# Mixers' driver: a longer modelled wait ahead of each unit's second-chunk transposition

## The chip, the cores and the metric

One core of one Trainium2 chip runs the whole program. The metric is the device time of one execution in microseconds (us). The kernel before took 2300.38 us as the median of three runs (2298.58 to 2304.85).

## What is computed

Two transformer blocks on 256 tokens of width 2048, in float32. The first block begins with two mixers that share one input projection; their outputs are concatenated and projected. The mixers are where the change lies:

```python
xn = _rmsnorm(h, norm_mix[l])
y = xn @ w_in[l]
o_gdn = _gdn_group(y[..., :GDN_COLS], ...)      # gated delta rule, 8 heads of 128
o_rwkv = _rwkv_group(y[..., GDN_COLS:], ...)    # RWKV-7 scan, 16 heads of 64
h = h + jnp.concatenate([o_gdn, o_rwkv], axis=-1) @ w_out[l]
...
# _gdn_group, behind the recurrence: norm of each head, gain, gate
o = o * lax.rsqrt(jnp.mean(o * o, axis=-1, keepdims=True) + NORM_EPS)
o = o * norm_w.astype(jnp.float32) * jax.nn.silu(z)
# _rwkv_group, behind the recurrence: norm of each head, gain and bias, bonus, gate
o = ((o - mean) * lax.rsqrt(var + RWKV_GN_EPS)).reshape(B, T, W) * ln_w + ln_b
return (o + bonus.reshape(B, T, W)) * g
```

Cross attention, a squared-ReLU MLP and a second block with two kinds of attention follow; the change does not touch them.

## The kernel before, in words

**The two recurrences** are computed in chunks of 128 tokens (two chunks), each with a triangular inverse in place of the token loop. The work is cut into six units: four RWKV quarters of four heads (`rwkv_quarter`, here q0 to q3) and two GDN halves of four heads (`gdn_half`, here g0 and g1). They run in the order q0, q1, g0, q2, q3, g1. Every unit has three stages, divided by `yield None`:

- Stage 0 makes the decayed operands and the matrices to be inverted (`pn` in a quarter, `gram` in a half, both into `nt`).
- Stage 1 (`inverse_blocks`) inverts the 32x32 diagonal blocks on POOL: four DMAs to DRAM (`scr`), four back (`nb`), then 31 pairs of a product `Xt<-X,nb` and a sum `X<-X,Xt`.
- Stage 2 puts the inverse into place (`by_row`, `xd`; `inverse`, whose products are `py` and `pz`), and then does chunk 0 and chunk 1. In a quarter every head and chunk needs a product `lp`, whose copy is masked by two affine selects on POOL (tiles `p2a`, `p2b`, `p2c`, `og` for the four heads) before the product `rp` reads it. Then come `up` and `op`. The result of a chunk is normed: sums on DVE, the power -1/2 on POOL (`powc`, L182, tiles `var` in a quarter and `sso` in a half), and a product on DVE (`oc` in a quarter, `og` in a half). Last, `finish(c)` transposes the chunk on PE (`onp` in a quarter, `ot` in a half) into the tile `mix`.

**The order on PE** is written by the program itself (`manual_schedule`). A driver keeps a modelled clock `now`. Each unit is a generator; it issues some matmuls and yields two numbers, the PE time of what it issued and the wait until its next piece may be issued:

```python
now += r[0]
stage[q][1] = now + r[1]
```

While no unit's piece is due, the driver issues pieces of `main()`, the big projections, whose products are called `acc` here (a piece is six products of 128x256, or three of 128x512, and counts 0.66). At most two units may be ahead of the last stage, and a unit enters a stage when the one before it has left. `main()` also names what it needs: before the first column strip of the cross attention's key projection is copied out, it waits for `("end", "q3")`. Where nothing is due and `main()` may not go on, the driver only moves its clock on, and PE gets nothing between the two pieces.

**The order on the other engines** (DVE, ACT, POOL, SP) is made by a scheduler that estimates times and takes PE's order as given. Each of these engines executes its instructions in that fixed order: an instruction that is not ready holds back what stands behind it. Weights arrive in pieces through three buffers: a DMA to `raw` (L130), a copy `whi` on ACT (L99), a difference `wlo` on DVE (L135).

Of the kernel before, what the change touches and what calls it, by code (L numbers as in the profile page):

```python
# [63 lines left out]
def block_kernel(tc, a, out, dbg=None, stop=99):  # L64
# [30 lines left out]
    def mm(o, l, r, start=True, stop=True):  # L95
        nc.tensor.matmul(o, l, r, start=start, stop=stop)  # L96

    def act(o, i, f=AF.Copy, **kw):
        return nc.scalar.activation(o, i, f, **kw)  # L99

    def tt(o, x, y, op, eng=None):
        (eng or nc.vector).tensor_tensor(out=o, in0=x, in1=y, op=op)  # L102

    def ts(o, x, s1, op0, s2=None, op1=None, eng=None):
        if op1 is None:
            (eng or nc.vector).tensor_scalar(out=o, in0=x, scalar1=s1, scalar2=None, op0=op0)
        else:
            (eng or nc.vector).tensor_scalar(out=o, in0=x, scalar1=s1, scalar2=s2, op0=op0, op1=op1)
# [6 lines left out]
    def pst(shape, name):  # L115
        return PS["pool"].tile(shape, F32, name=name, tag="ps", bufs=8 - PS["mm"])
# [63 lines left out]
    def powc(o, i, e):  # L180

        nc.gpsimd.tensor_tensor(out=o, in0=i, in1=e, op=ALU.pow)  # L182
# [177 lines left out]
    def wk(shape, name, bufs=1, dt=F32):  # L360
        return work_p.tile(shape, dt, name=name, tag=name, bufs=bufs)
# [192 lines left out]
    def rwkv_quarter(qt):  # L554
# [107 lines left out]
        def lmat(c, h):  # L662

            i, e = h // 2, slice(64 * (h % 2), 64 * (h % 2) + 64)
            lp = pst([128, 3, 128], "lp")
            mm(lp[:, 0, :], BK[e, i, c, 0, :], AR[e, i, c, 1, :])
            mm(lp[:, 1:3, :], BK[e, i, c, 1, :], AR[e, i, c, :, :])
            l = wk([128, 3, 128], ("p2a", "p2b", "p2c", "og")[h])
            act(l[:, 0, :], lp[:, 0, :], scale=rn2[:, c, h:h + 1])
            act(l[:, 1:3, :], lp[:, 1:3, :])  # L670

            nc.gpsimd.affine_select(out=l[:, 1, :], in_=l[:, 1, :], pattern=[[1, 128]],
                                    compare_op=ALU.is_ge, fill=0.0, base=-1, channel_multiplier=-1)
            nc.gpsimd.affine_select(out=l[:, 0:3:2, :], in_=l[:, 0:3:2, :], pattern=[[0, 2], [1, 128]],
                                    compare_op=ALU.is_ge, fill=0.0, base=0, channel_multiplier=-1)
            L[h] = l
# [10 lines left out]
        def finish(c):  # L687
            onp = pst([128, 2, 128], "onp")
            for i in range(2):
                tr(onp[:, i, :], oc[c][:, 2 * i:2 * i + 2, :].rearrange("p h n -> p (h n)"))  # L690
            s = slice(c * 128, c * 128 + 128)
            for i, ct in enumerate(cts):
                act(m[:, i, s], onp[:, i, :], AF.Identity, scale=p_lw[:, ct:ct + 1], bias=p_lb[:, ct:ct + 1])
            tt(m[:, :, s], m[:, :, s], bon[:, :, s], ADD)
            tt(m[:, :, s], m[:, :, s], gT[:, :, s], MUL)

        for c in range(2):
            rp_ = pst([128, 4, 64], "rp_")
            for h in range(4):
                if c == 1 and h % 2 == 0:  # L700
                    mm(rp_[:, h:h + 2, :], AR[:, h // 2, 1, 0, :], zs[:, h // 2, :], stop=False)
                mm(rp_[:, h, :], L[h][:, 1, :], vtok[:, c, h, :], start=(c == 0), stop=(c == 0 or h % 2 == 1))
            rs = wk([128, 4, 64], "rs")
            act(rs, rp_)
            yield 0.45 + 0.4 * c, 1.3
            up = pst([128, 4, 64], "up")
            for h in range(4):
                mm(up[:, h, :], tinv[:, c * 4 + h, :], rs[:, h, :])
            us = wk([128, 4, 64], "us")
            nc.vector.tensor_copy(us, up)  # L710
            yield 0.45, 1.5
            op = pst([128, 4, 64], "op")
            for h in range(4):
                if c == 1 and h % 2 == 0:
                    mm(op[:, h:h + 2, :], AR[:, h // 2, 1, 1, :], zs[:, h // 2, :], stop=False)
                mm(op[:, h, :], L[h][:, 0, :], us[:, h, :], start=(c == 0), stop=False)
                mm(op[:, h, :], L[h][:, 2, :], vtok[:, c, h, :], start=False, stop=(c == 0 or h % 2 == 1))
            if c == 0:
                zp = pst([128, 2, 64], "zp")
                for h in range(4):  # L720
                    i, e = h // 2, slice(64 * (h % 2), 64 * (h % 2) + 64)
                    mm(zp[e, i, :], btok[:, h, :], us[:, h, :], stop=False)
                    mm(zp[e, i, :], ktok[:, h, :], vtok[:, 0, h, :], start=False)
                for h1 in range(2):
                    e = slice(64 * h1, 64 * h1 + 64)
                    tt(zs[e, :, e], zp[e], zsc[e].unsqueeze(2).to_broadcast([64, 2, 64]), MUL)

            mean = wk([128, 4], "mean", bufs=2)
            nc.vector.tensor_reduce(out=mean, in_=op, axis=AX.X, op=ADD)
            ts(mean, mean, 1.0 / 64, MUL)  # L730
            o_ = wk([128, 4, 64], "oc")
            oc.append(o_)
            tt(o_, op, mean.unsqueeze(2).to_broadcast([128, 4, 64]), SUB)
            osq = wk([128, 4, 64], "rs")
            act(osq, o_, AF.Square)
            var = wk([128, 4], "var", bufs=2)
            nc.vector.tensor_reduce(out=var, in_=osq, axis=AX.X, op=ADD)
            ts(var, var, 1.0 / 64, MUL, 64e-5, ADD)
            powc(var, var, mhalf[:, 0:4])
            tt(o_, o_, var.unsqueeze(2).to_broadcast([128, 4, 64]), MUL)  # L740
            if c == 0:
                yield 1.5, 0.5
                for h in range(4):
                    lmat(1, h)
                    yield 0.65, 0.4 if h < 3 else 2.5
                finish(0)
                yield 0.22, 0
            else:
                yield 0.9, 7.0
                finish(1)  # L750
                yield 0.22, 0
        done.add(("end", f"q{qt}"))
# [33 lines left out]
    def gdn_half(hf):  # L786
# [118 lines left out]
        def finish(c):  # L905
            p = pst([128, 4, 128], "ot")
            for i in range(4):
                tr(p[:, i, :], o_[c][:, i, :])
            act(mix[hf][:, :, c * 128:c * 128 + 128], p)
# [33 lines left out]
        tt(o_[1], p, o_[1], ADD)  # L943
        norm(1)
        done.add(("gq", hf))
        yield 2.2, 9.0
        finish(1)
        done.add(("gz", hf))
        yield 0.45, 0
# [3 lines left out]
    def main():  # L953
# [85 lines left out]
        for n in range(4):  # L1039
            def emit_v(t, p, n=n):  # L1040
# [6 lines left out]
    res = {}  # L1047

    queue = [(("r", 0), rwkv_quarter(0)), (("r", 0), rwkv_quarter(1)), (("q", 0, "in"), gdn_half(0)),
             (("r", 1), rwkv_quarter(2)), (("r", 1), rwkv_quarter(3)), (("q", 1, "in"), gdn_half(1))]  # L1050
    stage = [None, None, None]
    now, need, ms = 0.0, None, main()
# [439 lines left out]
```

## Time and profile before

| | |
|---|---|
| median of three runs | 2300.38 us |
| the profiled execution | 2295.65 us |
| its span in the trace | 2293.9 us |
| PE busy | 2234.1 us, 97% of the span |
| DVE, ACT, POOL busy | 1389.2, 1122.2, 264.1 us |
| mean granted TensorE clock | 0.989 |
| PE waiting before `onp` in all | 7.3 us, 3 times |
| PE waiting before `ot` in all | 3.7 us, 2 times |

PE is the engine that is nearly always at work, and the mixers' units lie between 100 and 625 us of the span. What counts there is each stretch in which PE stands still, and the clock that it is granted afterwards. A wait shown behind a row in square brackets is the time in which the engine sat idle before that row, with the instruction that ended it.

### The profile page before, as it was taken

What the parts mean: (1) busy time and instruction counts of PE and PEld (TensorE: products, weight loads), DVE (VectorE), ACT (ScalarE), POOL (GpSimd) and SP (SyncE); (2) the same over time, 40 slices, a digit from 0 to 9 for tenths busy, and PEclk for the clock granted to TensorE, in tenths of its full rate; (3) what the DMA queues carried; (4) which work ended last, traced back from release to release, by engine and by line L of the source; (5) the groups of instructions that cost most, each with busy time, mean ns of one, the idle gap of its engine ahead of it and who ended that gap; (6) DMA issues with size and microseconds to landing.
All of it is one profiled execution on the core that took longest, in us unless ns stands there. A gap on an engine that the chain in (4) does not pass through costs nothing.

```text
span 2293.9 us, 39047 instructions
## 1 busy us (share of the span) xinstructions
PE 2234.1 (97%) x15506; PEld 2024.6 (88%) x15506; DVE 1389.2 (61%) x2236; ACT 1122.2 (49%) x1802; POOL 264.1 (12%) x540
## 2 busy tenths in 40 slices
PE   8999999989999999999999999999999999999996
PEld 8998988878988899889998898899888999889975
DVE  6575676675654556555554455455456677778765
ACT  5454544554544445444454444344344565656542
POOL 0036164155100000000000000000000000011101
PEclk9999999999999999999999999999999999999998
DMA  6654344343466554466666666666656666665654
GB/s 208 184 160 122 93 132 137 105 147 104 141 213 207 182 180 148 142 188 184 185 186 188 188 188 188 186 190 185 187 185 201 201 189 185 182 180 168 180 181 133
DMA packets 229060, 391.77 MB, mean 171 GB/s; under 512 B 39886, under 2 KB 47820, under 8 KB 228493
## 3 DMA queue, kind: packets, MB, share of 16 engines
q1 hardware_dynamic: 227297, 385.63, 55.9%
q10 hardware_dynamic: 1036, 3.58, 0.4%
q8 instruction: 121, 1.98, 0.4%
q14 instruction: 62, 0.51, 0.1%
q0 software_dynamic: 544, 0.07, 0.0%
HBM read 386.25 MB, written 2.97 MB: 170 GB/s over the span
## 4 chain that ended last, share of the span: by engine, by line
PE 85%; POOL 6%; DVE 3%; DMA 2%; issue 2%; ACT 1%; SPq 0%; POOLq 0%; ACTq 0%; DVEq 0%
PE acc L96 77%; POOL Xt L102 3%; POOL X L102 2%; PE lp L96 1%; DVE wlo L135 1%; DMA nb<-scr 1%; PE s2p L96 1%; PE o2p L96 1%; PE tp L178 1%; PE t2p L178 1%; PE xo L96 0%; PE xs L96 0%; DVE h L111 0%; DVE xd L494 0%; PE op L96 0%
## 5 line engine op out<-in xcount | busy, mean ns | idle before, releaser
L135 DVE TENSOR_TENSOR wlo<-raw,whi 128x1024 fp32r<-128x1024 f32 (+1 forms) x696 | 853.7, 1228 | 717.2 <-ACT whi L99 714.0
L99 ACT ACTIVATE whi<-raw 128x1024 fp32r<-128x1024 f32 (+1 forms) x696 | 734.5, 1056 | 875.2 <-PE acc L96 759.5
L96 PE MATMUL acc<-ah,whi 128*128 128x256 f32 x3120 | 885.9, 284 | 2.2 <-DVE ey L102 2.0
L96 PE MATMUL acc<-al,whi 128*128 128x256 f32 x3120 | 875.3, 281 | 0.0
L96 PE MATMUL acc<-ah,wlo 128*128 128x256 f32 x3120 | 871.2, 280 | 1.1 <-DVE wlo L135 1.1
L96 PEld LDWEIGHTS acc<-ah,whi 128*128 128x128 f32 x3120 | 588.8, 189 | 10.9 <-issue 6.3
L96 PEld LDWEIGHTS acc<-al,whi 128*128 128x128 f32 x3120 | 588.2, 189 | 1.4 <-issue 0.9
L96 PEld LDWEIGHTS acc<-ah,wlo 128*128 128x128 f32 x3120 | 586.5, 188 | 2.0 <-DVE wlo L135 1.9
L96 PE MATMUL acc<-wlo,ah 128*128 128x512 f32 x704 | 278.9, 397 | 0.0
L96 PE MATMUL acc<-whi,al 128*128 128x512 f32 x704 | 278.7, 397 | 0.0
L96 PE MATMUL acc<-whi,ah 128*128 128x512 f32 x704 | 268.7, 402 | 4.0 <-DVE qky L102 2.6
L96 PE MATMUL acc<-wlo,uh 128*128 128x512 f32 x512 | 202.4, 395 | 0.0
L96 PE MATMUL acc<-whi,ul 128*128 128x512 f32 x512 | 202.3, 395 | 0.0
L96 PE MATMUL acc<-whi,uh 128*128 128x512 f32 x512 | 182.5, 395 | 0.0
L96 PEld LDWEIGHTS acc<-whi,ah 128*128 128x128 f32 x704 | 132.5, 189 | 34.6 <-DVE qky L102 2.8
L96 PEld LDWEIGHTS acc<-whi,al 128*128 128x128 f32 x704 | 132.7, 189 | 31.9
L96 PEld LDWEIGHTS acc<-wlo,ah 128*128 128x128 f32 x704 | 133.0, 189 | 30.1
L96 PEld LDWEIGHTS acc<-whi,ul 128*128 128x128 f32 x512 | 96.1, 188 | 23.3
L96 PEld LDWEIGHTS acc<-wlo,uh 128*128 128x128 f32 x512 | 96.0, 188 | 23.3
L96 PEld LDWEIGHTS acc<-whi,uh 128*128 128x128 f32 x512 | 95.9, 187 | 23.3
L102 POOL TENSOR_TENSOR Xt<-X,nb 128x60 f32<-128x60 f32 (+24 forms) x186 | 82.0, 441 | 181.6 <-DMA nb<-scr 160.9
L1335 POOL MEMSET klz<- 64x256 f32 x8 | 2.5, 307 | 714.9 <-DMA raw<-in_w_in_dram 714.6
(523 smaller groups left out, 1873.4 us busy)
## 6 DMA issues: line engine op xcount, KB each, us to landing
raw<-in_w_in_dram SPq DMA_DIRECT2D x240, 512.0 KB, 3.7
raw<-in_mlp_w_up_dram SPq DMA_DIRECT2D x128, 512.0 KB, 3.7
raw<-in_mlp_w_down_dram SPq DMA_DIRECT2D x128, 512.0 KB, 3.9
raw<-in_w_out_dram SPq DMA_DIRECT2D x64, 512.0 KB, 4.8
raw<-in_xattn_wk_dram SPq DMA_DIRECT2D x32, 512.0 KB, 4.2
raw<-in_xattn_wv_dram SPq DMA_DIRECT2D x32, 512.0 KB, 5.4
raw<-in_xattn_wq_dram SPq DMA_DIRECT2D x32, 512.0 KB, 4.0
raw<-in_xattn_wo_dram SPq DMA_DIRECT2D x32, 512.0 KB, 4.3
```

The lines of the kernel that those rows point to most:

```text
L96: nc.tensor.matmul(o, l, r, start=start, stop=stop)
L99: return nc.scalar.activation(o, i, f, **kw)
L102: (eng or nc.vector).tensor_tensor(out=o, in0=x, in1=y, op=op)
L135: last["dve"] = nc.vector.tensor_tensor(out=lo, in0=raw, in1=hi.bitcast(F32), op=SUB)
L178: nc.tensor.transpose(o, i, ident[0:n, 0:n])
L1335: nc.gpsimd.memset(kl[other, e, :].bitcast(F32), 0.0)
```

## The change

Two numbers of the driver's model: the wait between the last norm of a unit and the transposition of its second chunk goes from 7.0 to 10.0 in a quarter (L749) and from 9.0 to 13.0 in a half (L946).

```diff
@@ rwkv_quarter
             else:
-                yield 0.9, 7.0
+                yield 0.9, 10.0
                 finish(1)
                 yield 0.22, 0
@@ gdn_half
         done.add(("gq", hf))
-        yield 2.2, 9.0
+        yield 2.2, 13.0
         finish(1)
         done.add(("gz", hf))
```

No instruction is added or removed: what changes is the order. On PE the stretch of `acc` products between the last product of a unit's chunk 1 and its second transposition has these lengths (products before, now): q0 66, 96; q1 66, 96; g0 84, 120; q2 66, 96; q3 66, 42; g1 84, 120. At q3 it becomes shorter: `main()` comes to its need for q3's end, and the driver has nothing else to issue. Since a unit's end now comes later, the units behind it enter their stages later too, and the scheduler sorts the other engines anew. Two places follow on which the prediction rests.

POOL, from the second masked head of q3's chunk 0 on, before. `p2b`, `p2c` and `og` are the masked tiles of heads 1, 2 and 3; `wB` and `z` belong to g1, and `Xt<-X,nb` is the first step of g1's inversion.

```order
L672 AFFINE_SELECT p2b<-p2b 128x128
L674 AFFINE_SELECT p2b<-p2b 128x2x128
L102 TENSOR_TENSOR wB<-wB,cst 128x512
L672 AFFINE_SELECT p2c<-p2c 128x128
L674 AFFINE_SELECT p2c<-p2c 128x2x128
L672 AFFINE_SELECT og<-og 128x128
L674 AFFINE_SELECT og<-og 128x2x128
L102 TENSOR_TENSOR z<-z,normw 128x512
L102 TENSOR_TENSOR Xt<-X,nb 128x31
```

The same place now:

```order
L102 TENSOR_TENSOR wB<-wB,cst 128x512
L672 AFFINE_SELECT p2b<-p2b 128x128
L674 AFFINE_SELECT p2b<-p2b 128x2x128
L102 TENSOR_TENSOR Xt<-X,nb 128x31
L102 TENSOR_TENSOR X<-X,Xt 128x31
L102 TENSOR_TENSOR Xt<-X,nb 128x30
L102 TENSOR_TENSOR X<-X,Xt 128x30
L102 TENSOR_TENSOR Xt<-X,nb 128x29
L102 TENSOR_TENSOR X<-X,Xt 128x29
L672 AFFINE_SELECT p2c<-p2c 128x128
L674 AFFINE_SELECT p2c<-p2c 128x2x128
L102 TENSOR_TENSOR Xt<-X,nb 128x28
```

Before, all four heads were masked ahead of g1's inversion. Now six of its steps stand ahead of `p2c`, and twelve more ahead of `og`.

DVE, at the end of g0's chunk 1, before. The first row waits for the power of g0's norm on POOL; `og<-og,sso,z` are the four products that the transposition `ot` waits for; `xd` are copies of q2's inverse and `gv` belongs to a projection.

```order
L102 TENSOR_TENSOR sso<-sso,rqd 128x4
L494 COPY xd<-Xt 32x8x8 x6
L111 SCALAR_TENSOR_TENSOR gv<-ey,par_250,gv 128x254
L494 COPY xd<-Xt 32x8x8 x5
L111 SCALAR_TENSOR_TENSOR gv<-ey,par_250,gv 128x254
L111 SCALAR_TENSOR_TENSOR og<-og,sso,z 128x128 x2
L135 TENSOR_TENSOR wlo<-raw,whi 128x1024
L111 SCALAR_TENSOR_TENSOR og<-og,sso,z 128x128 x2
```

The same place now:

```order
L102 TENSOR_TENSOR sso<-sso,rqd 128x4
L135 TENSOR_TENSOR wlo<-raw,whi 128x1024
L111 SCALAR_TENSOR_TENSOR gv<-ey,par_250,gv 128x254
L111 SCALAR_TENSOR_TENSOR gv<-ey,par_250,gv 128x255
L111 SCALAR_TENSOR_TENSOR og<-og,sso,z 128x128 x4
L111 SCALAR_TENSOR_TENSOR gv<-ey,par_250,gv 128x253
```

The copies of q2's inverse now stand behind g0's four products instead of between them. In both orders the power of this norm stands on POOL behind all 62 steps of q2's inversion. The power of q2's own last norm stands behind 22 steps of q3's inversion (16 before), and that of q3's last norm behind all 62 steps of g1's, as before.

## Rows read from the trace of the kernel before

**Rows 1.** The page, busy time of each engine.

```profile
PE 2234.1 (97%) x15506; PEld 2024.6 (88%) x15506; DVE 1389.2 (61%) x2236; ACT 1122.2 (49%) x1802; POOL 264.1 (12%) x540
```

**Rows 2.** Waits of PE between 100 and 625 us: total, times, longest.

```profile
PE onp L178 <- DVE oc L102: 7.3, 3, 3.7
PE ot L178 <- DVE og L111: 3.7, 2, 2.6
PE rp__2783 L96 <- POOL og L672: 2.7, 1, 2.7
PE rp__2783 L96 <- POOL p2c L672: 2.2, 1, 2.2
```

**Rows 3.** Timeline of PE at the ends of q1, g0, q2, q3 (start, us).

```profile
308.64 0.44 PE L178 MATMUL onp<-cst,oc 128*128 128x128 f32 x2 [0.89 <-DVE oc L102]
...
396.69 0.59 PE L178 MATMUL ot<-cst,og 128*128 128x128 f32 x2 [2.63 <-DVE og L111]
398.36 0.74 PE L178 MATMUL ot<-cst,og 128*128 128x128 f32 x2 [1.07 <-DVE og L111]
...
463.99 0.69 PE L178 MATMUL onp<-cst,oc 128*128 128x128 f32 x2 [3.66 <-DVE oc L102]
...
552.01 0.39 PE L96 MATMUL op<-p2d,og 128*128 128x64 f32 x2
...
562.97 0.44 PE L178 MATMUL onp<-cst,oc 128*128 128x128 f32 x2 [2.75 <-DVE oc L102]
```

**Rows 4.** Timeline of POOL: steps of inversions (X, Xt) and powers (L182).

```profile
391.41 1.02 POOL L182 TENSOR_TENSOR sso<-sso,cst 128x4 f32<-128x4 f32 x1
...
455.34 0.24 POOL L102 TENSOR_TENSOR Xt<-X,nb 128x31 f32<-128x31 f32 x1 [13.37 <-DMA nb<-scr]
...
462.35 1.02 POOL L182 TENSOR_TENSOR var<-var,cst 128x4 f32<-128x4 f32 x1
...
530.27 0.24 POOL L102 TENSOR_TENSOR Xt<-X,nb 128x31 f32<-128x31 f32 x1 [2.81 <-DMA nb<-scr]
...
536.95 0.34 POOL L102 TENSOR_TENSOR X<-X,Xt 128x69 f32<-128x69 f32 x1
...
548.51 1.33 POOL L102 TENSOR_TENSOR X<-X,Xt 128x75 f32<-128x75 f32 x1
...
561.44 1.02 POOL L182 TENSOR_TENSOR var<-var,cst 128x4 f32<-128x4 f32 x1
```

**Rows 5.** Timeline of DVE at q3's chunk 1.

```profile
548.42 1.22 DVE L135 TENSOR_TENSOR wlo<-raw,whi 128x1024 fp32r<-128x1024 f32 x1
...
555.89 0.17 DVE L108 TENSOR_SCALAR var<-var 128x4 f32<-128x4 f32 x1
...
562.49 0.43 DVE L102 TENSOR_TENSOR oc<-oc,var 128x256 f32<-128x256 f32 x1 [4.27 <-POOL var L182]
```

**Rows 6.** Stretches: us, busy by engine, PEclk, DMA share, GB/s.

```profile
213.50:220.30 6.80, 5.25 (x24) 5.25 (x25) 0.26 (x1) 0.38 (x1) 5.33 (x21) 0.50 0.17 62
397.80:401.20 3.40, 2.84 (x13) 2.77 (x14) 3.34 (x9) 0.90 (x2) 0.00 (x0) 0.50 0.52 154
462.60:469.40 6.80, 5.41 (x26) 5.42 (x27) 2.60 (x4) 1.86 (x3) 5.86 (x14) 0.50 0.16 54
559.00:566.00 7.00, 4.25 (x37) 4.05 (x36) 3.51 (x9) 2.71 (x4) 2.83 (x10) 1.00 0.32 101
...
495.00:521.00 26.00, 23.28 (x222) 19.06 (x221) 22.39 (x66) 17.10 (x41) 9.39 (x10) 1.00 0.36 115
```

**Rows 7.** Timeline of PE at q3's chunk 0 and g1's last gram.

```profile
516.82 0.92 PE L96 MATMUL lp<-wA,wB 64*128 64x128 f32 x4
517.67 0.49 PE L96 MATMUL gram<-gk 128*128 128x128 f32 x2
...
525.87 0.33 PE L96 MATMUL rp__6514<-p2d,p2a 128*128 128x64 f32 x2
```

**Rows 8.** Waits of PE between 1750 and 2294 us: total, times, longest.

```profile
PE o2p L96 <- ACT ph L99: 2.6, 3, 1.1
```

## Prediction

> **What bounds the kernel now.** I read the page first: PE is busy for 97% of the span [rows 1], so time can be won almost only where PE stands still, or runs at the lower clock. The second view is the list of PE's waits in the mixers' stretch. The reader is to see there that the largest are exactly those that the change aims at: 7.3 us before `onp` and 3.7 us before `ot` [rows 2]. The next two belong to one place, the product `rp` of q0, which waited 2.2 and 2.7 us for masks on POOL. The third view is PE's timeline, which says where the 11 us lie: 0.89 us at the end of q1, 2.63 and 1.07 us at g0, 3.66 us at q2, 2.75 us at q3 [rows 3]. q0 and g1 have no wait there. The fourth is the timeline of POOL and DVE beside them. At q3 the sums of the norm are ready at 555.89 + 0.17 = 556.06 us [rows 5], but POOL raises them to their power only at 561.44 [rows 4], because the last steps of g1's inversion stand before it; DVE then lost 4.27 us on that power [rows 5]. At q2 the power stands behind 16 inversion steps, which begin when their DMA has landed at 455.34 and end at 462.35 [rows 4]. So what PE waits for is mostly POOL's queue. The last view is a table of stretches: after the waits at q0 (4.9 us), g0 (3.7) and q2 (3.66) the granted clock was 0.50, that is 1.2 GHz, for 6.8, 3.4 and 6.8 us, and after q3's 2.75 us it stayed at 1.00, 2.4 GHz [rows 6].
>
> **What the longer waits take away.** A product of 128x256 takes PE about 0.12 us here: from the last `op` pair at 552.01 to the point at which the wait before `onp` began, 562.97 - 2.75 = 560.22, PE did that pair and 66 of them in 8.21 us [rows 3]. 30 more are 3.6 us, 36 more are 4.4 us. This work stands in the order anyway; it is only drawn ahead, so it costs nothing by itself.
>
> - q0 and g1: no wait before, nothing won.
> - q1: 3.6 us against 0.89, -0.9.
> - g0: 4.4 us against 3.70, -3.7. Its power stands behind the whole of q2's inversion (sso at 391.41, [rows 4]), and q2 enters its stages later now. But on DVE the copies of q2's inverse have moved out of the way, which gives some of that back. Bounds: -3.7, or -1.5 if the power is 2 us later.
> - q2: 3.6 us against 3.66, and six of the products are twice as wide; -3.7. The six more steps before the power cost some 3 us of POOL (16 took 7.0 us), but the norm itself comes later on PE against q3's inversion. Bounds -3.7 and -1.
> - The stretches at the lower clock behind g0's and q2's waits go with them. PE was busy 2.84 and 5.41 us in them, and half of that is lost [rows 6]: -1.4 and -2.7.
>
> **q3, where the order does the opposite.** Here PE gets 42 products instead of 66, 2.9 us less. If nothing else moved, its wait would grow to 2.75 + 2.9 = 5.6 us. But something moves: g1's inversion now stands earlier against q3 on POOL. In the new order 18 of its 62 steps come before the last mask of chunk 0, and 12 are left behind the last mask of chunk 1, so I expect it to be over when q3's last norm comes. Then the sums at 556.06, a power of 1.02 us and a product of 0.43 us [rows 4, 5] give 557.5 on the scale of before, and PE arrives at 552.2 + 42 x 0.12 = 557.3. Left over 0.3 us: -2.5.
>
> **What comes in its place.** The masks of q3's heads 2 and 3 in chunk 0 now stand behind 6 and 18 steps of an inversion whose first step cannot begin before its DMA has landed. `rp` reads them, and PE waits in order.
>
> - The first step began at 530.27, 12.6 us after g1's last gram at 517.67; the 18th ended at 536.95 + 0.34, so 18 took 7.0 us [rows 4, 7]. With the masks of head 2 and 3 in between (some 1 us) the last one is ready 12.6 + 8.0 = 20.6 us after that gram.
> - `rp` began 8.2 us after that gram at 525.87 [rows 7]. In the new order more stands between the two on PE: 36 products of 128x256 more and 6 of 128x512 fewer (net +2.9 us), two masked heads more (0.85 us each, from `lp` at 516.82 to the gram at 517.67, [rows 7]), and two small groups, 0.7 us. So `rp` comes about 13.5 us after it, and the product that needs the last mask 0.6 us later.
> - The wait: 20.6 - 14.1 = 6.5 us. Bounds: 3 us if the inversion's input is ready 3.4 us earlier, 9 us if the DMA lands 2.5 us later. The nearest row is q0's `rp`, with 4.9 us in the same position [rows 2]. I take 6.5.
> - The lower clock behind it, as after q0's: 5.25 us of work at half speed [rows 6], +2.6.
>
> The second block's attention is also sorted anew; there a transposed score stands directly before its product where 1.6 us of work stood between. Such places waited 2.6 us in 3 times [rows 8]: +0.9. The waits of PE for DVE between 495 and 521 us, where DVE is busy for 22.39 of 26 us [rows 6], I leave as they are: the same instructions are there in another order. Bounds -3 and +3.
>
> **The sum.** Won: 0.9 + 3.7 + 3.7 + 1.4 + 2.7 + 2.5 = 14.9 us. Lost: 6.5 + 2.6 + 0.9 = 10.0 us. Net -4.9 us. The profiled execution took 2295.65 us, 4.73 us (0.2%) less than the median, and less than the fastest of the three runs; the sum is a difference, so I set it against the median: 2300.4 - 4.9 = 2295.5 us, -0.2%.
>
> **A rule beside a row.** At 548.51 a step of the inversion took 1.33 us where its neighbours take 0.3, and DVE's `wlo` of 1.22 us had begun 0.1 us before it [rows 4, 5]. The Trainium skill, in SBUF — State Buffer, section Who interferes with whom, has it that a DVE instruction with two SBUF inputs contends with a GpSimd instruction that reads SBUF. The trace agrees, with that 1.33 us. By the rule each `wlo` within the 18 steps would add about 1 us to the wait of 6.5 us. My 7.0 us holds one slow step, as q0's stretch does; with two more, as a full stream of weight pieces would bring, the sum would be -2.9 instead of -4.9 us. I keep -4.9, since PE stands still there and new pieces stop when their three buffers are full.
>
> **The rivals.**
>
> - *Faster: the new wait is short.* In the order of before, DVE held the halves' `nt` products behind a slow power of POOL; in the new order the first four stand ahead of it. If that starts g1's inversion 3.4 us earlier, `rp` waits 3.1 us, which is less than the 3.66 that brought the lower clock and near the 2.75 that did not. Net: -14.9 + 0.9 + 3.1 = -10.9, 2289.5 us. For it: DVE is nearly full there. Against it: DVE's backlog also holds what follows. Chance 0.37.
> - *Slower: DVE takes the head start.* If DVE sets the pace between 495 and 521 us, PE comes there earlier and leaves as late as before, so all won before that point (0.9 + 3.7 + 3.7 + 1.4 + 2.7 = 12.4) is lost, while the new wait stays: -4.9 + 12.4 = +7.5, 2307.9 us. It decides when DVE has no idle time left; it had 3.6 of 26 us, and more before 495. Chance 0.09.
> - *The change does not do at q3 what it says.* The wait there was to be longer and is shorter in work. If g1's inversion is not over in time, the wait is 5.6 us instead of 0.3, with 2.7 us for the clock: -4.9 + 8.0 = +3.1, 2303.5 us. Against it: the steps that are left behind the masks. Chance 0.07.
>
> **How the numbers follow.** My forecast has 0.47. About 0.3%, 6.9 us, is what a measurement of this kernel can tell from no change. Forecast and third rival lie within it, less 0.02 for the forecast's tails, so the same has 0.52; faster has 0.38, the first rival and a tail; slower has 0.10, the second rival and a tail. The range reaches from just past the first rival to just past the third, 2288.0 to 2304.5 us, and leaves the second out.
>
> **What would show it.** In the changed profile the waits before `onp` and `ot` should be nearly gone in all (under 1.5 us of 11), q3's `rp` should wait 3 to 9 us for the masks `p2c` and `og` on POOL, and a stretch of lower clock should stand behind it, while none stands behind the ends of g0 and q2. g1's first inversion step should come before q3's `rp`, and its last one before q3's last power. I am wrong if `rp` does not wait, if an `onp` or `ot` still waits over 2 us, or if the waits for DVE around g1's grams grow by more than 3 us.

## The result, and the profile after

The changed kernel took 2284.66 us (median of 6 executions) against 2299.5 us for the kernel before (also 6): a ratio of 0.993 with a 95% interval of 0.9908 to 0.9953. It is faster by 0.7%, which is 14.8 us by the medians and 16 us by the ratio. I had said 2295.5 us, with 2288.0 as the lower end of the range: too slow, and outside it. The profiled execution took 2280.86 us, 0.2% under its median, as that of before was under its own; the two traces can be set side by side, and differ by 14.8 us of span.

The page of the changed kernel, busy time of each engine, to set against [rows 1]:

```profile
PE 2227.9 (98%) x15506; PEld 2019.4 (89%) x15506; DVE 1388.3 (61%) x2236; ACT 1120.6 (49%) x1802; POOL 260.7 (11%) x540
```

PE is busy for 6.2 us less with the same 15506 matmuls, in part because it ran less at the lower clock: half of its busy time in all such stretches of the trace is 10.4 us, against 14.2 before. The list of PE's waits between 100 and 625 us (total, times, longest) answers to [rows 2]:

```profile
PE rp__2783 L96 <- POOL og L672: 3.8, 1, 3.8
PE rp__6556 L96 <- POOL og L672: 1.5, 1, 1.5
PE pz L96 <- DVE y L511: 1.0, 2, 0.8
PE tp L178 <- ACT p2a L99: 0.8, 1, 0.8
PE onp L178 <- DVE oc L102: 0.8, 1, 0.8
PE rp__2783 L96 <- POOL p2c L672: 0.8, 1, 0.8
PE ot L178 <- DVE og L111: 0.6, 1, 0.6
```

The 11.0 us before `onp` and `ot` are 1.4 (0.8 at q3's end, and 0.6 before the transposition of g0's first chunk). q0's `rp` (here `rp__2783`) waits as before, 4.6 us against 4.9. The new wait, at q3's `rp` (`rp__6556`), is 1.5 us where I had put 6.5. The whole list adds up to 11.5 us; that of before to 20.8.

PE's timeline at the ends of q1, g0, q2 and q3, for [rows 3], with g1's last gram and q3's `rp` between them, for [rows 7]:

```profile
313.04 0.38 PE L178 MATMUL onp<-cst,oc 128*128 128x128 f32 x2
...
396.88 1.12 PE L178 MATMUL ot<-cst,og 128*128 128x128 f32 x4
...
463.05 0.38 PE L178 MATMUL onp<-cst,oc 128*128 128x128 f32 x2
...
498.08 0.46 PE L96 MATMUL gram<-gk 128*128 128x128 f32 x2 [0.50 <-DVE al L111]
...
515.52 0.33 PE L96 MATMUL rp__6556<-p2d,p2a 128*128 128x64 f32 x2
...
517.77 0.43 PE L96 MATMUL rp__6556<-p2d,og 128*128 128x64 f32 x2 [1.48 <-POOL og L672]
...
549.48 0.44 PE L178 MATMUL onp<-cst,oc 128*128 128x128 f32 x2 [0.79 <-DVE oc L102]
```

q1, g0 and q2 end without a wait there, q3 with 0.79 us. The last mask was ready, and its product began, 19.7 us after that gram (517.77 - 498.08). But PE reached `rp` 17.4 us after it, not 13.5. The timeline of POOL shows the mask about 1 us before I expected it, and g1's inversion over before q3's last power, for [rows 4]:

```profile
509.96 0.24 POOL L102 TENSOR_TENSOR Xt<-X,nb 128x31 f32<-128x31 f32 x1 [2.93 <-DMA nb<-scr]
...
512.68 1.13 POOL L102 TENSOR_TENSOR X<-X,Xt 128x28 f32<-128x28 f32 x1
...
517.42 0.29 POOL L672 TENSOR_SCALAR_AFFINE_SELECT og<-og 128x128 f32<-128x128 f32 x1
...
540.78 0.22 POOL L102 TENSOR_TENSOR X<-X,Xt 128x8 f32<-128x8 f32 x1
546.06 1.02 POOL L182 TENSOR_TENSOR var<-var,cst 128x4 f32<-128x4 f32 x1 [5.06 <-DVE var L108]
```

Last the table of stretches (us, busy time of PE, PEld, DVE, ACT, POOL, granted clock, DMA share, GB/s), for [rows 6]:

```profile
212.30:219.10 6.80, 6.08 (x28) 6.08 (x29) 0.42 (x1) 0.38 (x1) 4.67 (x19) 0.50 0.06 23
396.50:399.90 3.40, 3.40 (x26) 2.88 (x25) 3.40 (x10) 1.80 (x3) 0.00 (x0) 1.00 0.47 154
459.00:465.80 6.80, 6.78 (x50) 6.05 (x49) 5.84 (x9) 3.38 (x6) 6.25 (x9) 1.00 0.41 116
505.70:509.10 3.40, 3.40 (x22) 3.18 (x22) 1.09 (x3) 0.60 (x2) 0.66 (x2) 0.53 0.49 154
```

At the ends of g0 and q2 the clock stays at 1.00 (2.4 GHz) now. There is a stretch at 0.53 in front of q3's `rp`, at 505.7, which I had not seen coming; it is part of why PE came there late.

### The profile page after: what moved, and what is told of

It reads as the page before. It is cut to its first block, busy times and chain, and to the rows that moved or that the text cites. A ratio compares the mean times of both kernels' runs of the same rounds, so it can differ in the third digit from the quotient of the medians.

```text
span 2279.1 us, 39049 instructions
## 1 busy us (share of the span) xinstructions
PE 2227.9 (98%) x15506; PEld 2019.4 (89%) x15506; DVE 1388.3 (61%) x2236; ACT 1120.6 (49%) x1802; POOL 260.7 (11%) x540
## 4 chain that ended last, share of the span: by engine, by line
PE 88%; DVE 4%; POOL 3%; DMA 2%; ACT 2%; issue 1%; SPq 0%; DVEq 0%; POOLq 0%; ACTq 0%
PE acc L96 79%; POOL X L102 2%; POOL Xt L102 1%; DVE wlo L135 1%; PE lp L96 1%; DMA raw<-in_w_in_dram 1%; PE op L96 1%; PE o2p L96 1%; PE s2p L96 1%; PE t2p L178 1%; ACT whi L99 1%; PE xo L96 0%; PE xs L96 0%; PE tp L178 0%; DMA nb<-scr 0%
## 5 line engine op out<-in xcount | busy, mean ns | idle before, releaser
L102 POOL TENSOR_TENSOR Xt<-X,nb 128x60 f32<-128x60 f32 (+24 forms) x186 | 71.9, 386 | 175.1 <-DMA nb<-scr 154.7
```

## The experiments

My theory (A): the time is won place by place, from the waits at the ends of units and the lower clock behind them, and lost at `rp`, where masks stand in POOL's queue. Rivals are named with the runs. Ratios are to the kernel before on the same chip. Where the mean granted clock of several executions is given, its lack to 1, times the span, is called the time at the lower clock; it is an upper estimate, since PE has no work in part of that time.

**One half of the change at a time.**

The quarters' wait alone, on the kernel before:

```diff
-                yield 0.9, 7.0
+                yield 0.9, 10.0
```

> The quarters' wait alone is 10.0, the halves' stays 9.0. Theory A (the time comes place by place from the waits at the ends of units and the lower clock behind them): q1's wait of 0.9 us goes; g0's 3.7 us before ot and the lower clock behind it stay as in the kernel before; q2's power now stands behind 35 steps of the next inversion (16 before, 22 with both waits changed), so q2's onp still waits, 2 to 7 us, with the lower clock behind it; the masks of q3's chunk 0 stand before g1's inversion, so q3's rp does not wait. In all -1 to -5 us, ratio 0.998 to 1.000. Theory B (the gain comes from the new sorting of the other engines as a whole, not from the ends): the ends' waits do not tell the time; either most of the 0.7% is here, or the kernel is slower although q1's wait is gone.

Measured: 2294.5 us, 0.9968 (0.9949 to 0.9987). PE's waits between 100 and 640 us:

```profile
PE ot L178 <- DVE og L111: 5.2, 2, 4.5
PE ssg L96 <- ACT tha L99: 3.3, 1, 3.3
...
PE onp L178 <- DVE oc L102: 1.7, 1, 1.7
```

The halves' wait alone, on the kernel before:

```diff
-        yield 2.2, 9.0
+        yield 2.2, 13.0
```

> The halves' wait alone is 13.0, the quarters' stays 7.0. Theory A: g0's 3.7 us before ot shrink below 1 us and the lower clock behind them goes (-1.4); q1's 0.9 us and q2's 3.66 us before onp with the 2.7 us of lower clock stay; q3's rp waits under 2 us, since its last mask of chunk 0 stands behind 7 steps of g1's inversion only. In all about -5 us, ratio 0.998. Theory B: as in the other run, the sum of the ends' waits does not tell the time.

Measured: 2292.67 us, 0.9954 (0.9937 to 0.9972). PE's waits between 100 and 625 us, and one stretch:

```profile
PE onp L178 <- DVE oc L102: 2.9, 2, 1.7
...
PE ot L178 <- DVE og L111: 0.4, 1, 0.4
```

```profile
416.90:427.10 10.20, 10.20 (x43) 7.34 (x42) 4.46 (x13) 3.10 (x7) 1.26 (x4) 0.51 0.01 2
```

Each half wins, and -0.32% and -0.46% make -0.78%, near the -0.70% of both. So the total adds up, but my detail did not hold, and both ratios lie below what I had put. q2's last `onp` has no wait in either run, though with the quarters' wait alone its power stands behind 35 steps of the next inversion, and with the halves' alone its own wait is the old 7.0. In the first, that inversion began at 451.84 us and the power came at 468.98, while `onp` stood only at 474.0; in the second it began at 461.47, with the power at 468.3. How many steps stand in front says little; when the first of them can begin says it. In exchange each run has costs of its own: in the first 3.3 us of waiting for ACT before `ssg`, in the second 10.2 us at the lower clock from 416.9.

Theory B is not refuted by these two runs. The listed waits fall from 20.8 us to 16.7 and 17.7, that is by 4.1 and 3.1 us, while the medians fall by 9.4 and 11.2. The clock can be what is missing: its mean is 0.9858 over 29 executions of the kernel before, and 0.9882 and 0.9896 over 12 of each half, which is up to 5.7 and 8.7 us less at the lower clock. So in either trace the waits alone are less than half of the gain.

**The same order up to q3, executed three times.** One run undoes the change for q3 alone, which leaves PE's order up to and past q3's last `onp` as it is in the changed kernel; the other is the changed kernel itself.

```diff
-                yield 0.9, 10.0
+                yield 0.9, 10.0 if qt < 3 else 7.0
```

> The changed kernel with q3's wait back at 7.0. Theory A (at q3 the wait is without effect, because the driver has nothing else to place there until q3 ends): onp of q3 has the same 42 products before it and waits the same 1 us, q3's rp waits 1 to 2 us, and the time is that of the changed kernel, ratio 0.993 within 0.003. Rival D: q3's longer wait carries part of the gain by what it places behind onp (30 products stand elsewhere); then the ratio moves to 0.996 or more.

> The changed kernel itself, once more. Theory H (the waits at one place, and the lower clock there, differ from execution to execution under one and the same order): q3's rp waits 1.2 to 3.5 us, the lower clock stretch of 3.4 us ahead of it may or may not be there, and its presence goes with the shorter wait; ratio 0.993 within 0.003. Rival: the order fixes both; rp waits 1.5 us again, with the 3.4 us of lower clock before it.

Measured: 2287.75 us, 0.9942 (0.9923 to 0.996) without the change at q3; 2285.89 us, 0.9922 (0.9899 to 0.9946) for the changed kernel again. PE's timeline at g1's last gram and q3's `rp`, and two stretches, of the run without the change at q3:

```profile
502.68 0.46 PE L96 MATMUL gram<-gk 128*128 128x128 f32 x2 [0.50 <-DVE al L111]
...
518.66 0.33 PE L96 MATMUL rp__6556<-p2d,p2a 128*128 128x64 f32 x2
...
522.62 0.43 PE L96 MATMUL rp__6556<-p2d,og 128*128 128x64 f32 x2 [3.18 <-POOL og L672]
```

```profile
502.70:518.60 15.90, 14.14 (x182) 11.85 (x183) 11.01 (x24) 5.74 (x15) 8.62 (x18) 1.00 0.32 85
522.80:526.20 3.40, 3.40 (x18) 3.40 (x19) 0.84 (x1) 1.44 (x2) 2.85 (x9) 0.52 0.00 0
```

And of the changed kernel again, the same two views:

```profile
503.46 0.46 PE L96 MATMUL gram<-gk 128*128 128x128 f32 x2 [0.50 <-DVE al L111]
...
525.47 0.33 PE L96 MATMUL rp__6556<-p2d,p2a 128*128 128x64 f32 x2
...
526.09 0.39 PE L96 MATMUL rp__6556<-p2d,og 128*128 128x64 f32 x2
```

```profile
416.10:419.50 3.40, 3.40 (x60) 3.11 (x60) 2.83 (x9) 0.87 (x3) 0.88 (x2) 0.50 0.18 71
511.70:525.40 13.70, 13.70 (x72) 11.71 (x71) 3.20 (x5) 2.34 (x5) 8.44 (x27) 0.50 0.28 78
```

One order, three outcomes. PE came to `rp` 16.0 us after the gram with no lower clock in between, and waited 3.2 us; 17.4 us after it with 3.4 us of lower clock, and waited 1.5 us; 22.0 us after it with 13.7 us of lower clock, and did not wait (I had put 1.2 us as the least). So theory H holds: what PE loses at the lower clock it need not wait at `rp`, and the order alone fixes neither. That q3's own wait has no effect on the products at its place, as theory A had it, is in the order already: the driver has nothing else to put there. Whether it wins something behind `onp` (rival D) is not settled, since the two ratios overlap; I had put `rp`'s wait at 1 to 2 us there, and it was 3.2.

**More products in front of q3's `rp`.**

```diff
-            yield 0.65, lat - 0.65
+            yield 0.65, lat - 0.65 + (3.0 if h == 4 and qt == 3 else 0.0)
```

> The changed kernel with q3's first rp 3 us later in the driver: 24 more products of 0.12 us stand before it (36 instead of 12), and 18 instead of 42 before its last onp; all before it stands as in the changed kernel. Theory A (the last mask comes about 20 us after g1's last gram whatever PE does, and PE's own delays had eaten my 6.5 us of wait): rp waits 0 to 0.6 us instead of 1.5 to 3.3, onp waits 1 to 4 us instead of 0.6 to 0.95, and the time stays within 0.3% of the changed kernel, ratio 0.991 to 0.997. By the numbers of my prediction (PE there 14.1 us after that gram, mask at 20.6) rp would still wait 3.6 us.

Measured: 2295.07 us, 0.9977 (0.9962 to 0.9991). PE's timeline, and the stretch behind the last row:

```profile
520.01 0.33 PE L96 MATMUL rp__6591<-p2d,p2a 128*128 128x64 f32 x2
...
521.78 0.43 PE L96 MATMUL rp__6591<-p2d,og 128*128 128x64 f32 x2 [0.99 <-POOL og L672]
...
558.07 0.69 PE L178 MATMUL onp<-cst,oc 128*128 128x128 f32 x2 [3.85 <-DVE oc L102]
```

```profile
557.00:563.80 6.80, 5.73 (x27) 5.73 (x28) 1.28 (x3) 0.90 (x3) 0.56 (x1) 0.51 0.24 77
```

`rp` waits 1.0 us, 2.2 less than the 3.2 of the undisturbed order, for 24 products that are worth 2.8; nearer to theory A (0 to 0.6) than to the 3.6 us of my prediction's numbers. The products were taken from in front of `onp`, which now waits 3.85 us and is followed by the lower clock. The ratio is above the 0.997 that I had put as the highest. I had not foreseen that `rp` of q3's second chunk waits 1.6 and 0.7 us for its masks on POOL at 542 us, with 3.4 us of lower clock behind; the changed kernel has no wait there. At q3 PE has a fixed stock of products until the quarter ends, and moving 24 of them forward cost some 9 us.

**Longer still.**

```diff
-                yield 0.9, 10.0
+                yield 0.9, 13.0
-        yield 2.2, 13.0
+        yield 2.2, 17.0
```

> Both waits longer still: 13.0 and 17.0. The order now puts 120, 108 and 81 products before the last onp of q0, q1 and q2, and 156 before the last ot of g0 and g1, but none before q3's. Theory A (a wait at an end is what the norm needs less the work in front): nothing more to win at q0, q1, q2, under 1 us at g0; at q3 the 42 products of the changed kernel (4.9 us) are gone from the place where 0.95 us of wait was left, so onp waits 5 to 7 us with the lower clock (about 3 us) behind it: +5 to +9 us against the changed kernel, ratio to before 0.995 to 0.998. Theory E (longer waits hide more everywhere): 0.993 or less.

Measured: 2310.81 us, 1.0043 (1.0018 to 1.0067). PE's timeline at q3's last `onp`, and the stretch behind:

```profile
578.16 0.69 PE L178 MATMUL onp<-cst,oc 128*128 128x128 f32 x2 [7.17 <-DVE oc L102]
```

```profile
572.10:582.30 10.20, 4.14 (x20) 4.14 (x21) 5.43 (x21) 4.96 (x13) 1.02 (x1) 0.50 0.00 0
```

The place and the mechanism were right, the size too small: besides the 7.2 us here, q3's `rp` waits 2.5 and 2.5 us for masks, and a product of `main()` waits 3.8 us for `z` on DVE, which I did not foresee. Rival E falls: longer is not better everywhere. Of the three settings that were run, 10.0 and 13.0 is the fastest.

**The masks out of POOL's queue.** `strict` is a constant made once (`tri` less the identity).

```diff
+            if c == 0 and h >= 2:
+                tt(l[:, 1, :], l[:, 1, :], strict, MUL)
+                tt(l[:, 0:3:2, :], l[:, 0:3:2, :], tri.unsqueeze(1).to_broadcast([128, 2, 128]), MUL)
+            else:
             nc.gpsimd.affine_select(...)
```

On the changed kernel, and on the kernel before:

> The changed kernel, with the masks of heads 2 and 3 in chunk 0 applied on DVE as products with a constant, out of POOL's queue. Theory A (rp waits because the masks stand behind steps of an inversion on POOL): q0's rp waits under 0.5 us instead of 4.6, the lower clock behind it (half of 6.2 us of work, 3.1 us) goes, q3's rp does not wait (1.5): -9 us against the changed kernel, ratio to before 0.989. Theory C (PE only meets the next late thing there: the inverse's copies or the activation that ends the L matrices): q0's rp or up still waits 2 us or more for ACT or DVE, and the time stays within 0.3% of the changed kernel, ratio 0.992 to 0.994. Cost either way: 4 products of DVE a quarter, 0.35 to 0.42 us each.

> The kernel before (waits of 7.0 and 9.0) with the masks of heads 2 and 3 in chunk 0 on DVE. Theory A: q0's rp loses its 4.9 us and the lower clock behind it (2.6 to 3.1), the waits at g0, q2 and q3 stay (3 to 4 us each): about -8 us, ratio 0.9965, and the two edits add up (0.993 times 0.9965 is 0.9895). Rival: the masks only pay together with the longer waits; ratio 0.999 or more.

Measured: 2277.58 us, 0.9896 (0.987 to 0.9922) on the changed kernel; 2292.31 us, 0.996 (0.9945 to 0.9976) on the kernel before. Stretches of the first:

```profile
209.00:219.00 10.00, 10.00 (x93) 9.38 (x92) 4.91 (x10) 2.87 (x4) 8.45 (x23) 1.00 0.34 91
503.00:516.70 13.70, 13.70 (x71) 11.71 (x71) 4.46 (x9) 2.34 (x5) 8.75 (x27) 0.50 0.27 78
```

q0's `rp` does not wait, and the lower clock behind it is gone, in both: POOL's queue was the cause there, and theory C falls. For q3's `rp` these runs show less: with the longer waits it does not wait, but 13.7 us at the lower clock stand before it, and behind such a stretch it did not wait in the changed kernel either; on the kernel before it waits 1.1 us, now for a mask on DVE. The edits add up (0.993 times 0.996 is 0.989), so the rival that the masks only pay with the longer waits falls too. No run was measurably faster than this one, about 7 us under the changed kernel, though its profiled execution had 13.7 us at the lower clock from 503.

**The waits around g1's last grams.** With the masks on DVE, 3.1 us are left there before `bkp`, `gram`, `tp` and `pz`. I took work from DVE: copies of the inverse to POOL; the products `wB` to ACT and POOL; the copy of `vp` to ACT as well.

```diff
-                        nc.vector.tensor_copy(o, i_)
+                        (nc.gpsimd if (q + b) % 2 else nc.vector).tensor_copy(o, i_)
```

> The changed kernel with the masks on DVE, and 8 of the 12 copies of each inverse (32x64, 0.23 us each) moved from DVE to POOL. Theory F (the waits of 0.7 to 1 us before bkp, gram, tp and pz around g1's last grams are DVE's backlog there, and the lower clock behind them comes with them): DVE has 1.9 us less to do between 486 and 489 us, these waits fall from 3.4 to under 2 us in all; against the masks alone -1.5 to -8 us, ratio to before 0.986 to 0.989. Rival G (the copies are slower on POOL, or the chain behind them waits for the last one): py or lp waits 1 us or more for POOL in several units, and the time is no better, 0.9896 or more.

```diff
-                    stt(at[:, q, :], p[:, j, 1, :], cs[...], gam[:, c, i + j, :], MUL, MUL)
+                    act(at[:, q, :], p[:, j, 1, :], scale=cs[...])
+            tt(at[:, 4 * c:4 * c + 4], at[:, 4 * c:4 * c + 4], gam[:, c], MUL, eng=nc.gpsimd)
```

> The changed kernel with the masks of heads 2 and 3 on DVE, and with the decayed products wB of each half formed by ACT (from PSUM, scaled) and POOL (times the decay) instead of by 8 DVE products of 0.26 us. Theory F (the waits of 3.3 us in all before bkp, gram, tp and pz at g1's last grams come from the 12 us without a pause on DVE that begin with a weight piece at 485 us): DVE has 2.1 us less in that very stretch, these waits fall below 2 us, and the lower clock of 13.7 us behind them shrinks; -1.5 to -8 us against the masks alone, ratio to before 0.986 to 0.989. Rival: ACT becomes what they wait for (its queue is full between 480 and 495 us), ratio 0.9896 or more.

> As the run with wB on ACT and POOL, and the copy of vp (0.68 us on DVE) on ACT as well. Theory F: the waits fall by another 0.3 to 0.6 us, ratio 0.985 to 0.989. Rival: ACT is late with the masks' input instead, and tp or rp waits more than 1 us for ACT; no better than 0.9896.

Measured: 2277.73 us, 0.9898 (0.988 to 0.9916); 2279.01 us, 0.989 (0.9859 to 0.9921); 2280.18 us, 0.9895 (0.9868 to 0.9922). None can be told from the masks alone. Without the copies DVE only paused 0.92 us for a weight piece that ACT had not copied yet, and the waits stayed at 2.8 us. With `wB` elsewhere they were 2.5 us, with `vp` as well 2.6, and ACT took DVE's place. Theory F had put them under 2 us; its cause is not shown (waits of PE between 100 and 640 us, second run):

```profile
PE lp L96 <- ACT p2e L99: 1.6, 1, 1.6
PE bkp L181 <- ACT wB L99: 0.9, 1, 0.9
```

**The kernel before, once more.**

> The kernel before once more, to tell what belongs to its order and what to one execution. Order: the waits before onp and ot (q1 0.9, g0 2.6 and 1.1, q2 3.7, q3 2.8, each within 0.5 us), q0's rp (4.9), and the lower clock behind g0 and q2. Execution: the lower clock at 414.8 us that has no wait before it, and the first 200 us; if the stretch at 414.8 is absent here, its 1.7 us are no term of the change; if it is there again, I left out a term that the order sets.

Measured: 2304.28 us, one execution. Waits of PE between 100 and 640 us, and stretches:

```profile
PE onp L178 <- DVE oc L102: 6.6, 3, 3.6
PE ot L178 <- DVE og L111: 3.9, 3, 2.5
```

```profile
416.10:419.50 3.40, 3.40 (x20) 3.17 (x20) 1.92 (x5) 1.49 (x3) 0.92 (x2) 0.52 0.00 0
425.00:433.20 8.20, 8.20 (x62) 7.06 (x60) 4.30 (x12) 3.70 (x9) 0.66 (x2) 1.00 0.26 79
433.20:450.30 17.10, 17.10 (x72) 12.94 (x71) 5.09 (x13) 6.58 (x18) 3.78 (x9) 0.50 0.29 86
472.80:479.60 6.80, 6.80 (x61) 6.80 (x61) 3.31 (x4) 3.19 (x5) 5.86 (x13) 1.00 0.27 77
569.70:573.10 3.40, 3.40 (x18) 3.40 (x18) 2.83 (x8) 1.65 (x3) 0.00 (x0) 0.52 0.53 137
```

The waits are the order's: 10.5 us before `onp` and `ot` against 11.0, and the whole list 20.6 against 20.8 us, as the changed kernel's two lists add up to 11.5 and 11.8. The lower clock is not. It did not come behind q2's wait of 3.6 us this time (clock 1.00 from 472.8), came behind q3's wait of 2.4 us (569.7), where 2.75 us had brought none, and came for 17.1 us from 433.2. The stretch near 415 us came in both executions of the kernel before, and in one of two of the changed kernel.

## Why the prediction was wrong

| term | predicted | the two traces |
|---|---|---|
| waits before `onp` and `ot` | -10.8 | 11.0 to 1.4: -9.6 |
| lower clock behind g0 and q2 | -4.1 | gone: -4.1 |
| lower clock near 415 us | not in the sum | 3.40 / 2: -1.7 |
| q3's `rp` | +6.5 | +1.5 |
| lower clock there | +2.6 | 3.40 / 2: +1.7, in front of it |
| block 2's attention and what else waits behind 625 us | +0.9 | 13.0 to 13.6: +0.6 |
| lower clock behind q0's `rp` | 0 | (6.08 - 5.25) / 2: +0.4 |
| other waits from q0's `rp` to 625 us | 0 | -0.5 |
| before q0's `rp`, where PE's order is unchanged | 0 | 209.2 to 207.5: -1.7, of which 0.7 is a wait at 190.77 |

That is -13.4 of the 14.8 us by which the spans differ; the rest is neither in the listed waits nor in the lower clock.

- **The step that failed** is "So `rp` comes about 13.5 us after it". It came after 16.0 us even where the clock stayed up. I had taken the way from the trace of before and added work to it, but no wait. There PE has none between the gram and `rp`: it is busy for all 8.20 us; the waits for DVE that I left as they are all stand ahead of the gram. In the new order two stand behind it, 0.8 us at `tp`, for ACT, and 1.0 at `pz`, for DVE. The two small groups, for which I put 0.7 us, took 1.6 (0.62 for `py`, from 499.14 to 499.76, and 0.99 for `pz` with the group behind it, from 503.65 to 504.64). The other side was near: the mask came 19.7 to 21.0 us after the gram, where I had 20.6, with one slow step of the inversion among the 18 (1.13 us at 512.68, with a `wlo` begun at 512.49), as my 7.0 us held. So 6.5 us was 3.2, 1.5 or nothing, and the 2.6 us behind it were 1.7 in front, 1.7 behind, or 6.9 in front.

The way in the kernel before, and the two waits on it in the changed kernel:

```profile
517.67:525.87 8.20, 8.20 (x69) 6.62 (x69) 5.45 (x12) 4.29 (x10) 4.14 (x8) 1.00 0.26 65
```

```profile
501.47 0.66 PE L178 MATMUL tp<-cst,rT 128*128 128x128 f32 x4 [0.79 <-ACT p2a L99]
...
503.65 0.22 PE L96 MATMUL pz<-xt,y 32*32 32x32 f32 x2 [0.83 <-DVE y L511]
```

- **The lower clock** is the second term that was mis-sized: -4.1 and +2.6, together -1.5 us, each read from one execution. The mean granted clock is 0.9858 over 59 executions of the kernel before (0.9855 to 0.9859 in each of three batches) and 0.9897 over 12 of the changed one, which is up to 9 us less at the lower clock. The profiled execution of before, with 0.989, had less of it than most. At an equal clock of 0.990 five executions of before took 2293.5 to 2298.9 us and four of the changed kernel 2285.1 to 2287.4. By the medians that is 9.3 us, and 9 to 12 us at each of the four clocks (0.987 to 0.990) that both have. All their medians differ by 16.5 us (2302.2 and 2285.7), so by estimate 4 to 7 us of the gain go with the clock, where I had 1.5, and 9 to 12 with the waits and the rest, where I had -10.8 + 6.5 + 0.9 = -3.4.
- **The ends of units** came out within 1.2 us, q3 with 0.79 us left against my 0.3, and the lower clock behind g0 and q2 did not come. But I had read both from one execution; the clock behind q2 is not there in the second execution of the kernel before. That term happened to be right. Before q2's last `onp` the trace has 90 products, six of them twice as wide: the work of 96, and no more.
- **The rivals.** The first (2289.5 us, 0.37) is nearest, for another reason than mine: the inversion began 11.9 us after the gram instead of 12.6, not 3.4 us earlier; PE was later. The second did not happen: DVE did not take the head start. The third did not either: g1's inversion ended at 540.78 + 0.22, 5 us before q3's last power.
- **The size in all.** About 6 of the 10 us missed are at q3's `rp` and its clock in this pair of traces. Some 3 us more lie in the stretch near 415 us and in the first 209 us; both differ between executions of one kernel. Two pairs of traces have -9.3 and -8.8 us of listed waits before 625 us, near the 9.3 us at an equal clock, while the medians of the changed kernel's two batches say -14.8 and -16.3. The rest goes with the lower clock, which the new order gets less of. In part that goes with the waits that it took away; but the stretches near 415 and 433 us have no wait in the 13 us ahead of them, and why they come is open.

## What to carry to other kernels

When you cost a new wait, time both sides from the same event, and ask which waits the new order puts on the way of the side that arrives, even where the trace of before has none there: a late arrival pays for part of the wait. Before you cost the lower clock from one profile, compare that execution's granted clock with those of the others. A queue's length in steps is no delay; ask when its first step can begin. And where a place has a fixed stock of filler work, moving it forward only moves the wait: the masks' move to another engine took away 4.6 us and the lower clock behind it, while longer waits in the order turned into 7.2 us elsewhere.

## What I had not expected of the hardware

The lower clock (granted 0.50, 1.2 GHz) did not come with waits alone. It came at 433.2 us in the second execution of the kernel before, after 8.2 us in which PE was busy for all 8.20, and stayed for 17.1 us with PE busy throughout. And after a wait of 3.6 us it did not come. The Trainium skill (TensorE: Matmul & The Clock Gate, section What's actually happening) has the clock follow how busy PE has been recently; the first of these rows does not agree with that, by the busy time that the trace shows, and the second need not contradict it. Half of PE's busy time at the lower clock is 14.2 and 24.9 us in the two traces of the kernel before, 10.4 and 17.5 in those of the changed one; the differences of 10.7 and 7.1 us are at least as large as those of the spans, 8.7 and 7.1. The 59 executions of the kernel before say the same: the five that took longest (2313.4 to 2315.5 us) have a mean clock of 0.980 or 0.981, the five with 0.990 took 2293.5 to 2298.9.
